# Second layer of a three-layer block: keys transposed among the products of q, query stores on ScalarE's queue, the layer's end re-banked

## The chip, the cores and the metric

The kernel runs on one core of a Trainium2 chip. The core has five engines that run side by side: TensorE (PE, matrix products), VectorE (DVE), ScalarE (ACT), GpSimd (POOL) and SyncE (SP, which here only issues DMAs). The metric is the device time of one execution in microseconds, the median of several runs of the same program.

## What is computed

Three layers over a sequence of L = 1024 tokens of width D = 1024, in float32. The first (sliding-window attention beside a state-space mixer) and the third (a convolution, a second state-space mixer, a gated output) are untouched. The change lies in the second layer, sparse attention, and at the seam to the third:

```python
def odd_layer(hn, rel_bias, w_in, w_out, q_g, k_g):
    q, k, v, gate, qi, ki, wi = split_cols(hn @ w_in, ODD_SPLITS)
    q = rms_norm(q.reshape(bsz, L, C_HEADS, C_HEAD_DIM), q_g)      # 8 heads of 128
    k = rms_norm(k.reshape(bsz, L, C_KV_HEADS, C_HEAD_DIM), k_g)   # 2 heads of 128
    ...
    att = dsa_attention(q, k, v, qi, ki, wi, rel_bias)
    return (att * jax.nn.silu(gate)) @ w_out
```

In `dsa_attention` each query scores all earlier keys with the small index heads `qi`, `ki`, `wi`, keeps the 256 best, and attends to those alone. The layer's result is added to `h`, and the third layer begins with `h = layer_norm(x, ln_emb_g, ln_emb_b)` and one large product of that with `w_in`.

## The kernel before

**Products.** Every float32 operand of a product is split into a high and a low part, and a product of 128 tokens by 512 columns over one slice of the width takes three matrix instructions (`mm3`, L146 to L150). A tile of 128 tokens over the width of 1024 is 8 such triples, 24 instructions (`form1`, L152). Weights arrive in `wraw` by SP, ScalarE copies the high part (L122), GpSimd subtracts for the low part (L123). An instruction's place on its engine is found by a scheduler from priorities, and each engine works through its own list strictly in that order. SP and ScalarE issue DMAs in the same way: one that waits holds up all behind it.

**The k, v and q products** (`phase_b`, L828, from L926 to L958). A loop over eight token tiles makes k and v, 24 instructions each; `head_norm` (L389) copies k out of its bank (L397), squares it (L400), sums on VectorE (L402), forms the root on GpSimd (L168) and multiplies on GpSimd (L406). `keys(tt - 2)` then transposes the normalised k of the tile two back into `kTB` (L933, with a ScalarE scale at L935 and a VectorE split at L936); the last two follow the loop. Then come two halves `ch` of q, eight tiles each, through the same `head_norm`, whose last line (L410) stores the tile to the scratch tensor `d_q` from SP. The copies `qo` have two buffers. While these products run, `TopK` searches for the 256th largest score by bisection in all query blocks: VectorE counts for blocks 2 to 4, ScalarE for blocks 5 to 7 (L1076), 31 steps each, and `finish` (L1083) writes the mask with four long VectorE passes over a scratch tile `cum` (L1118 to L1121).

**The attention** (`DSA`). For each query block and half of the heads, `load` fetches q from `d_q` (L1137), transposes it (`tq`, L1141) and splits it (L1143, L1144). Scores `s` are products of `kTB` and `qTB`. Blocks go in the order 0, 1, 7, 6, 5, 4, 3, 2.

**The layer's end** (L981 to L1002). For each token tile, `out_tile` (L1008) makes columns 512 to 1023 of the output product from the split copies `ms` (L1019, L1020), loads the residual into `hr` (three buffers, L1027 and L1028), adds (L1030) and stores (L1031); `ln_tile` normalises; the tile goes to `d_h0` (L994) and is transposed in two halves into `hnTC`, the stationary or moving operand of the whole third layer. PSUM has eight banks, given out by `k.psum(mm=2, tp=1, sd=3, cy=2)`: the products use the three single banks `sd`, the transposes a two-bank tile `cyt` in one buffer (L995 to L1002).

**The third layer's start** (`phase_c`, L1237). `c_vectors` (L1448) loads short row vectors (L1455 to L1473) and transposes them (L1462, L1470, L1475); then products `pb` and `pa` (two banks `mm`) make the convolution's input, 48 instructions per pair, closed by a sigmoid on ScalarE (L1270) and a product on VectorE (L1271).

## Time and profile before

| | us |
|---|---|
| median of 3 runs | 2135.31 |
| lowest, highest | 2134.58, 2135.98 |
| the profiled execution | 2137.92 |
| its span | 2136.2 |

The profiled execution is one run with the hardware profiler on. Its span, from the first to the last record, is 1.7 us shorter than its own time. TensorE's mean granted clock over the span was 0.955 of full speed. A busy share is an average over stages; what an edit is worth is read in the stage where it lies, from the idle time of the engine that sets the pace there and from what ended that idle time. In the rows below, the name in brackets at the end of a row of a timeline is the idle time just before and the instruction that ended it.

### The profile page before, as it was taken

The numbers are of one execution on the slowest core, as the hardware profiler recorded it, in microseconds if no ns is written. First come the engines' busy times: TensorE is split into PE (matmuls) and PEld (weight loads), VectorE is DVE, ScalarE is ACT, GpSimd is POOL, SyncE is SP. The second block draws the span as 40 slices with busy tenths as digits, with TensorE's granted clock in tenths as the row PEclk, the third lists the DMA queues.
The fourth block names the chain that finished last, engine by engine and source line by source line (L and its number), as shares of the span: only waits on it lengthen the run. The fifth ranks groups of instructions, "written<-read, shape, count | busy, mean of one in ns | idle before, by whom it ended". The sixth has DMA issues, their size and how long they took to land. (4 is left out here: it accounts for less than half of the span.)

```text
span 2136.2 us, 27568 instructions
## 1 busy us (share of the span) xinstructions
PE 1942.1 (91%) x9291; PEld 1571.2 (74%) x9291; DVE 1518.4 (71%) x2995; ACT 846.9 (40%) x1604; POOL 906.7 (42%) x734
## 2 busy tenths in 40 slices
PE   8988899899999998899987799999999659999998
PEld 6777677777788777677856688788888537778786
DVE  8365504674479998598854299999997488857737
ACT  5223326564457885455554221133322411134210
POOL 5567416555322246464566131222232576643204
PEclk9989999999999999899999799999999869999999
DMA  6543332313222212733454132222433445574442
GB/s 196 157 123 106 108 126 86 115 38 114 75 65 70 65 50 81 236 132 119 134 168 156 46 111 78 70 89 80 127 121 106 148 139 171 165 239 175 157 158 99
DMA packets 166694, 256.19 MB, mean 120 GB/s; under 512 B 29078, under 2 KB 77548, under 8 KB 166554
## 3 DMA queue, kind: packets, MB, share of 16 engines
q1 hardware_dynamic: 156330, 236.62, 35.1%
q10 hardware_dynamic: 10224, 17.82, 2.3%
q8 instruction: 73, 1.20, 0.2%
q14 instruction: 67, 0.55, 0.1%
HBM read 185.35 MB, written 75.06 MB: 122 GB/s over the span
## 5 line engine op out<-in xcount | busy, mean ns | idle before, releaser
L123 POOL TENSOR_TENSOR w<-wraw,w 128x512 fp32r<-128x512 f32 (+1 forms) x230 | 313.2, 1376 | 674.7 <-ACT w L122 671.9
L1285 DVE SCALAR_TENSOR_TENSOR cy<-u,cw,cy 128x1024 f32<-128x1024 f32 x232 | 298.7, 1288 | 5.7
L122 ACT ACTIVATE w<-wraw 128x512 fp32r<-128x512 f32 (+1 forms) x230 | 141.4, 622 | 191.5 <-DMA wraw<-in_w_in_dram 53.3
L149 PE MATMUL mm<-hnTC,w 128*128 128x512 f32 (+1 forms) x336 | 131.6, 392 | 0.0
L150 PE MATMUL mm<-hnTC,w 128*128 128x512 f32 (+1 forms) x336 | 131.5, 391 | 0.0
L148 PE MATMUL mm<-hnTC,w 128*128 128x512 f32 (+1 forms) x336 | 131.5, 391 | 0.0
L1165 POOL TENSOR_TENSOR lgB<-lgB,sc 128x1024 f32<-128x1024 f32 (+5 forms) x48 | 84.4, 1788 | 75.7 <-DMA lgB<-d_T 73.1
L148 PE MATMUL mm<-w,ms 128*128 128x512 f32 x256 | 105.1, 410 | 10.1 <-ACT ms L1019 9.3
L150 PE MATMUL mm<-w,ms 128*128 128x512 f32 x256 | 105.5, 412 | 7.3 <-POOL ms L1020 6.9
L1076 ACT ACTIVATE tkj<-sc,tks 128x896 bf16<-128x896 f32 (+2 forms) x93 | 96.4, 1038 | 26.1 <-DVE tks L1072 23.8
L149 PE MATMUL mm<-w,ms 128*128 128x512 f32 x256 | 103.2, 403 | 1.4 <-POOL w L123 1.2
L168 POOL TENSOR_TENSOR hr<-hm,mhalf 128x2 f32<-128x2 f32 (+2 forms) x40 | 46.8, 1170 | 89.4 <-DVE hm L403 57.8
L148 PE MATMUL mm<-w,hnTA 128*128 128x512 f32 (+1 forms) x192 | 73.1, 384 | 7.8 <-DVE qo L406 7.8
L148 PE MATMUL mm<-hnTB,w 128*128 128x512 f32 (+2 forms) x208 | 78.4, 377 | 0.7 <-ACT hnTB L172 0.7
L149 PE MATMUL mm<-w,hnTB 128*128 128x512 f32 x192 | 77.5, 404 | 0.9 <-POOL w L123 0.9
L149 PE MATMUL mm<-hnTB,w 128*128 128x512 f32 (+2 forms) x208 | 78.1, 376 | 0.0
L150 PE MATMUL mm<-hnTB,w 128*128 128x512 f32 (+2 forms) x208 | 78.1, 375 | 0.0
L148 PE MATMUL mm<-w,hnTB 128*128 128x512 f32 x192 | 77.7, 406 | 0.0
L150 PE MATMUL mm<-w,hnTB 128*128 128x512 f32 x192 | 77.3, 403 | 0.0
L149 PE MATMUL mm<-w,hnTA 128*128 128x512 f32 (+1 forms) x192 | 73.3, 382 | 0.3 <-POOL w L123 0.3
L150 PE MATMUL mm<-w,hnTA 128*128 128x512 f32 (+1 forms) x192 | 73.3, 383 | 0.0
L148 PEld LDWEIGHTS mm<-hnTC,w 128*128 128x128 f32 (+1 forms) x336 | 61.6, 183 | 14.6
(609 smaller groups left out, 5899.2 us busy)
## 6 DMA issues: line engine op xcount, KB each, us to landing
wraw<-in_w_in_dram SPq DMA_DIRECT2D x56, 256.0 KB
wraw<-in_od_w_in_dram SPq DMA_DIRECT2D x48, 256.0 KB
wraw<-in_ev_w_in_dram SPq DMA_DIRECT2D x32, 256.0 KB
wraw<-in_w_in_dram SPq DMA_DIRECT2D x64, 128.0 KB
wraw<-in_w_out_dram SPq DMA_DIRECT2D x32, 256.0 KB
ld<-d_cs SPq DMA_DIRECT2D x16, 512.0 KB
hr<-h SPq DMA_DIRECT2D x24, 256.0 KB
d_T<-d_row SPq DMA_DIRECT2D x8, 576.0 KB
```

Source lines behind the costliest of these rows:

```text
L122: nc.scalar.activation(t[:, 0, :o], raw[:, :o], AF.Copy)
L123: nc.gpsimd.tensor_tensor(t[:, 1, :o], raw[:, :o], t[:, 0, :o].bitcast(F32), op=ALU.subtract)
L148: mm(out, aH, bH, start=start, stop=False)
L149: mm(out, aH, bL, start=False, stop=False)
L150: mm(out, aL, bH, start=False, stop=stop)
L168: self.nc.gpsimd.tensor_tensor(out, ms, self.mhalf[:, :n], op=ALU.pow)
L1076: S.activation(self.junk(n), sc[b], AF.Sign, bias=cand[:, i:i + 1], accum_out=cnt[:, i:i + 1])
L1165: G.tensor_tensor(lg[:, :n], lg[:, :n], self.masks[b], op=ALU.add)
L1285: V.scalar_tensor_tensor(py if i < 30 else y, u[:, i:i + L], cw[:, ct, i:i + 1], py, op0=ALU.mult, op1=ALU.add)
```

## The change

- `keys` is no longer called among the k, v products. It follows each q tile of the first half, and its transposes are tied behind that tile's last product (`k.last`, set in `mm3`) by `tc.issue_after`. The eight normalised k tiles wait in the two `rl` tiles (four of them) and in the tile `cum` (the other four), so the first `cum` pass of `TopK.finish` comes after the last key transpose.
- The stores to `d_q` leave SP. `head_norm` takes a callback `store`, called right after its ScalarE copy: tile t's store is issued by ScalarE after the copy of tile t + 1, and ScalarE waits there for GpSimd's multiplication of tile t.
- At the layer's end the output products use the two `mm` banks, the transposes the three `sd` banks, one half tile each (`to_hnT`, L175).
- `c_vectors` moves from ahead of the third layer's first products to behind the first pair of them, tied with `issue_after`. Lines after L147 are shifted by one to a few.

```diff
@@ mm3
-        mm(out, aL, bH, start=False, stop=stop)
+        self.last = mm(out, aL, bH, start=False, stop=stop)
@@ head_norm(..., o=None, store=None)
     if leave:
-        S.activation(o[:, :n], ps, AF.Copy)
-        ps = o[:, :n]
+        S.activation(o, ps, AF.Copy)
+        if store is not None:
+            store()
+        ps = o
@@ k, v and q products
-    def keys(tt, kn):
+    kn = [xp.tile([P, 512], F32, tag="rl", name="kn", bufs=2) for _ in range(2)]
+    kn.append(xp.tile([P, L], F32, tag="cum", name="kn", bufs=1))
+    def kraw(tt):
+        return kn[min(tt // 2, 2)][:, (tt % 2 if tt < 4 else tt - 4) * 256:][:, :256]
+    def keys(tt):
         pt = k.tp()
-        for j in range(2):
-            T.transpose(pt[:, j * P:(j + 1) * P], kn[:, j * P:(j + 1) * P], k.ident)
+        with tc.issue_after(k.last.ins):
+            for j in range(2):
+                T.transpose(pt[:, j * P:(j + 1) * P], kraw(tt)[:, j * P:(j + 1) * P], k.ident)
...
-        if tt > 1:
-            keys(tt - 2, kns[tt - 2])
-        if tt % 2 == 0:
-            kn2 = xp.tile([P, 512], F32, tag="rl", name="kn", bufs=2)
-        kns.append(head_norm(k, gp, ps[:, :256], 2, 128, None, True, kn2[:, tt % 2 * 256:tt % 2 * 256 + 256]))
-    for tt in range(NT - 2, NT):
-        keys(tt, kns[tt])
+        head_norm(k, gp, ps[:, :256], 2, 128, None, True, kraw(tt))
+    store = None
...
-            head_norm(k, gp, ps, 4, 128, d_q[tt * P:(tt + 1) * P, ch * 512:ch * 512 + 512], True)
+            if ch == 0:
+                keys(tt)
+            o = head_norm(k, gp, ps, 4, 128, None, True, None, store)
+            store = partial(nc.scalar.dma_start, d_q[tt * P:(tt + 1) * P, ch * 512:ch * 512 + 512], o)
+    store()
@@ the layer's end
-        h = out_tile(k, mo, op, tt, 1, [mix], wo, x, hout, bank="sd")
+        h = out_tile(k, mo, op, tt, 1, [mix], wo, x, hout)
...
-        cy = k.pp.tile([P, L], F32, tag="cy", name="cyt", bufs=1)
-        for hf in range(2):
-            c = cy[:, hf * 512:hf * 512 + 512]
-            for kk in range(4):
-                T.transpose(c[:, kk * P:(kk + 1) * P], h[:, (hf * 4 + kk) * P:(hf * 4 + kk + 1) * P], k.ident)
-            hs = slice(hf * 4, hf * 4 + 4)
-            k.split_bank(c.rearrange("p (k t) -> p k t", k=4), hnC[:, 0, hs, tt * P:(tt + 1) * P],
-                         hnC[:, 1, hs, tt * P:(tt + 1) * P])
+        k.to_hnT(h, hnC, tt, "sd")
@@ phase_c
-    c_vectors(k, up, cw, sw, dtx, sng)
...
                 k.form2(pa, hnT, th * 512, w, KT, m * P)
+                if j + th + m == 0:
+                    with tc.issue_after(k.last.ins):
+                        c_vectors(k, up, cw, sw, dtx, sng)
```

**SP's list at the q products.** `wraw` is a weight load, `lgB` a bias load of the attention. Before:

```order
L110 DMA wraw<-in_od_w_in_dram 128x512 x34
L410 DMA d_q<-qo 128x512 x6
L110 DMA wraw<-in_od_w_out_dram 128x512 x4
L410 DMA d_q<-qo 128x512
L110 DMA wraw<-in_od_w_out_dram 128x512 x3
L410 DMA d_q<-qo 128x512
L110 DMA wraw<-in_od_w_out_dram 128x512
L410 DMA d_q<-qo 128x512 x3
L1137 DMA qf<-d_q 128x512
L1163 DMA lgB<-d_T 128x128 x4
```

Now:

```order
L111 DMA wraw<-in_od_w_in_dram 128x512 x34
L111 DMA wraw<-in_od_w_out_dram 128x512 x8
L1138 DMA qf<-d_q 128x512
L1164 DMA lgB<-d_T 128x128 x4
L1138 DMA qf<-d_q 128x512
```

The eleven stores ahead of the first query load, and the five behind it, are gone from this list and stand in ScalarE's.

**VectorE's list where the mask of block 2 is finished** (`kTB<-` is the split of a key tile, `cum<-` the first passes of the mask, `tks_` and `hm` small steps of the search and of `head_norm`). Before:

```order
L936 SCALAR_TENSOR_TENSOR kTB<-tp,bg,kTB 128x2x128
L1107 TENSOR_TENSOR tks_7495<-tks_7495 128x3
L1072 TENSOR_SCALAR tks_7516<-tks_7516 128x1
L403 TENSOR_SCALAR hm<-hm 128x2
L1115 TENSOR_SCALAR tkj_7496,tks_7495<-sc_5062,tks_7495 128x384
L1116 TENSOR_SCALAR eq<-sc_5062,tks_7495 128x384
L1080 TENSOR_TENSOR tks_7542<-tks_7542 128x1
L1117 TENSOR_SCALAR tks_7495<-tks_7495 128x1
L1118 SCALAR_TENSOR_TENSOR cum<-mone,eq 128x384
```

Now:

```order
L1116 TENSOR_SCALAR tkj_7529,tks_7528<-sc_5066,tks_7528 128x896
L1118 TENSOR_SCALAR tks_7528<-tks_7528 128x1
L1081 TENSOR_TENSOR tks_7541<-tks_7541 128x1
L1119 SCALAR_TENSOR_TENSOR cum<-mone,eq 128x384
L1082 COPY_PREDICATED tks_7541<-tks_7541 128x1
L1120 SCALAR_TENSOR_TENSOR cum<-cum,tks_7494,eq 128x384
L1073 TENSOR_SCALAR tks_7541<-tks_7541 128x1
L946 SCALAR_TENSOR_TENSOR kTB<-tp,bg,kTB 128x2x128
L1121 TENSOR_TENSOR cum<-cum,tkj_7495 128x384
```

The `cum` passes of blocks 2, 3 and 4 stood behind the sixth of the eight key splits and now stand around the eighth, with those of blocks 5, 6 and 7 close behind; the last of block 7 stands directly ahead of the first query's split, as before.

**TensorE's list at the end of the layer** (its first row is the last of 24 products `pa`). Before:

```order
L150 MATMUL pa<-hnTC,w 128x512
L999 MATMUL cyt<-ident,hr 128x128 x4
L1462 MATMUL tp<-ident,rows 128x36 x8
L999 MATMUL cyt<-ident,hr 128x128 x4
L1470 MATMUL tp<-ident,rows_11079 128x5 x6
L1470 MATMUL tp<-ident,rows_11088 128x5 x6
L999 MATMUL cyt<-ident,hr 128x128 x4
L1475 MATMUL tp<-ident,rows_11098 128x8
L999 MATMUL cyt<-ident,hr 128x128 x16
```

Now:

```order
L151 MATMUL pa<-hnTC,w 128x512
L182 MATMUL tph<-ident,hr 128x128 x4
L1465 MATMUL tp<-ident,rows 128x36 x4
L182 MATMUL tph<-ident,hr 128x128 x4
L1465 MATMUL tp<-ident,rows 128x36 x4
L1473 MATMUL tp<-ident,rows_11184 128x5 x6
L1473 MATMUL tp<-ident,rows_11193 128x5 x6
L149 MATMUL pb<-hnTC,w 128x512
```

Of the last transposes of `hr` seven groups of four stood between the first pair of products and the second; now two do, and the one of L1475 stands inside the second pair. Between the last product of the output (`mm<-w,ms`) and these rows stand 36 products `pb` and `pa` and one group of `cyt` before, 34 products and two groups of `tph` now. In SP's list the load of `conf_conv_w` (L1455) stood directly behind the store of tile 6's sum (L1031) and now stands behind the store of the normalised tile 6 (L994); the two loads of the residual of tile 7 (L1027, L1028) stood behind the loads of the row vectors and now stand ahead of them, behind the store of the normalised tile 4.

## Rows read from the trace of the kernel before

**Rows 1.** The page, busy time by engine: us, share of the span, instructions.

```profile
PE 1942.1 (91%) x9291; PEld 1571.2 (74%) x9291; DVE 1518.4 (71%) x2995; ACT 846.9 (40%) x1604; POOL 906.7 (42%) x734
```

**Rows 2.** Stretches of the span: length, busy time by engine, granted clock, DMA.

```profile
core 0: us, PE busy (x) PEld busy (x) DVE busy (x) ACT busy (x) POOL busy (x), PEclk, DMA share, GB/s
1160.00:1180.00 20.00, 8.69 (x48) 6.81 (x46) 5.96 (x15) 5.08 (x9) 3.98 (x4) 0.68 0.32 109
1200.00:1300.00 100.00, 100.00 (x443) 82.81 (x442) 72.84 (x62) 16.69 (x26) 20.51 (x16) 1.00 0.26 82
```

**Rows 3.** TensorE's waits from 734 to 875 us: total, times, longest.

```profile
PE tp L933 <- POOL kn L406: 8.3, 2, 5.2
```

**Rows 4.** TensorE in time, k, v and q products: start, length, line, [idle <-releaser].

```profile
733.80 0.39 PE L150 MATMUL mm<-w,hnTB 128*128 128x512 f32 x1
739.39 0.69 PE L933 MATMUL tp<-ident,kn 128*128 128x128 f32 x2 [5.20 <-POOL kn L406]
...
837.69 0.39 PE L149 MATMUL mm<-w,hnTB 128*128 128x512 f32 x1
...
848.57 0.39 PE L149 MATMUL mm<-w,hnTB 128*128 128x512 f32 x1
857.42 1.12 PE L1141 MATMUL tq<-ident,qf 128*128 128x128 f32 x4 [8.46 <-DMA qf<-d_q]
...
872.60 0.22 PE L148 MATMUL s<-kTB,qTB 128*128 128x128 f32 x1
```

**Rows 5.** SP's queue in time, at the end of the products of q.

```profile
839.55 14.23 SPq L410 DMA_DIRECT2D d_q<-qo  x3
853.88 0.38 SPq L1137 DMA_DIRECT2D qf<-d_q  x1
```

**Rows 6.** Issuing one DMA from ScalarE (stores of d_gate), ns min/median/max.

```profile
L922 ACTq DMA_DIRECT2D d_gate<-gtB x16: 326/326/327, 609.1 to 718.5; - x16
```

**Rows 7.** Two stretches of the k, v and q products, columns of rows 2.

```profile
734.20:800.00 65.80, 57.50 (x243) 46.77 (x244) 65.61 (x281) 56.39 (x121) 26.98 (x28) 0.92 0.14 41
800.00:854.00 54.00, 48.06 (x209) 38.51 (x207) 47.17 (x122) 31.13 (x56) 35.66 (x26) 0.99 0.23 79
```

**Rows 8.** VectorE in time, the last block's top-k ends, first query follows.

```profile
847.68 2.28 DVE L1118 TENSOR_TENSOR_SCAN cum<-mone,eq 128x1024 f32<-128x1024 f32 x1
...
853.06 0.93 DVE L1121 TENSOR_SCALAR sc<-cum 128x1024 f32<-128x1024 f32 x1
...
859.29 0.75 DVE L1144 SCALAR_TENSOR_TENSOR qTB<-tq,bg,qTB 128x512 fp32r<-128x512 f32 x1 [1.23 <-ACT qTB L1143]
```

**Rows 9.** ScalarE's copy of a tile of q, and GpSimd's last step on it.

```profile
812.61 0.58 ACT L397 ACTIVATE qo<-mm 128x512 f32<-128x512 f32 x1
...
817.06 1.04 POOL L406 TENSOR_TENSOR qo<-qo,hr 128x512 f32<-128x512 f32 x1
```

**Rows 10.** TensorE in time, end of the second layer.

```profile
1154.14 0.39 PE L150 MATMUL mm<-w,ms 128*128 128x512 f32 x1
...
1172.55 0.61 PE L1462 MATMUL tp<-ident,rows 36*128 36x36 f32 x4 [8.93 <-DMA rows<-in_b_glu_dram]
...
1193.69 0.79 PE L148 MATMUL pb<-hnTC,w 128*128 128x512 f32 x1 [2.69 <-ACT stg L1270]
```

**Rows 11.** Residual adds (tiles 5, 6), GpSimd's end of tile 5's layer norm.

```profile
1140.64 0.68 DVE L1030 TENSOR_TENSOR hr<-mm,hr 128x512 f32<-128x512 f32 x1
...
1155.80 0.69 DVE L1030 TENSOR_TENSOR hr<-mm,hr 128x512 f32<-128x512 f32 x1 [4.93 <-DMA hr<-h]
...
1146.40 1.74 POOL L1229 TENSOR_TENSOR hr<-hr,bbC 128x512 f32<-128x512 f32 x1
```

**Rows 12.** SP's queue in time: loads of the row vectors.

```profile
1156.88 0.30 SPq L1455 DMA_DIRECT2D rows<-in_conf_conv_w_dram  x1
...
1165.21 0.25 SPq L1457 DMA_DIRECT2D rows<-in_conf_ln_g_dram  x1
...
1169.56 0.29 SPq L1458 DMA_DIRECT2D rows<-in_b_glu_dram  x1
```

More of the change, by code (lines that the diff above doesn't have):

```diff
@@ L1 @@
 from contextlib import ExitStack
+from functools import partial
 import math
@@ L386, in phase_a, with head_norm @@
     return hnT, sB
-def head_norm(k, pool, ps, nh, dh, dst, leave=False, o=None):
+def head_norm(k, pool, ps, nh, dh, dst, leave=False, o=None, store=None):
     nc = k.nc
@@ L394, in head_norm @@
     if o is None:
-        o = pool.tile([P, 512], F32, tag="qo", name="qo", bufs=2)
+        o = pool.tile([P, 512], F32, tag="qo", name="qo", bufs=2)[:, :n]
     if leave:
-        S.activation(o[:, :n], ps, AF.Copy)
-        ps = o[:, :n]
+        S.activation(o, ps, AF.Copy)
+        if store is not None:
+            store()
+        ps = o
     sq = pool.tile([P, 512], F32, tag="sq", name="sq", bufs=1)
@@ L405, in head_norm @@
     k.rstd(r[:, :nh], m[:, :nh], nh)
-    (G if leave else V).tensor_tensor(o[:, :n].rearrange("p (h d) -> p h d", h=nh),
+    (G if leave else V).tensor_tensor(o.rearrange("p (h d) -> p h d", h=nh),
                                       ps.rearrange("p (h d) -> p h d", h=nh),
@@ L409, in head_norm @@
     if dst is not None:
-        nc.sync.dma_start(dst, o[:, :n])
+        nc.sync.dma_start(dst, o)
     return o
@@ L937, in keys @@
                                op0=ALU.mult, op1=ALU.subtract)
-    kns = []
     for tt in range(NT):
```

## The prediction, made before the changed kernel ran

> **What bounds the kernel now.** I read the page first, then the windows, then TensorE's waits and its timeline at the two places that the change touches, and last the lists that release it there. TensorE is busy for 1942.1 of 2136.2 us [rows 1], so an edit is worth the TensorE idle time (or half-clock time) that it removes, where nothing else takes its place. Behind the second place TensorE is full: 100.00 of 100.00 us from 1200 on [rows 2]. What is gained before 1200 therefore reaches the end; nothing later can absorb it. The sum is made against the profiled execution, 2137.92 us, which is 2.6 above the median 2135.31; I take the 2.6 off at the end. From no change a measurement here tells about 0.2%, 4.3 us.
>
> First place, the k, v and q products. TensorE stops for the keys: it stood 5.20 us at 739.39, 8.3 in two stops [rows 3, 4], because the k of two tiles back had not yet passed `head_norm` on GpSimd. It stops again 8.46 us before the query transpose at 857.42, for a load of q [rows 4]. Nothing was slow in that load. SP stood 14.23 us in three stores of q, each waiting for GpSimd's multiplication, and the load was issued directly behind them, at 853.88 [rows 5]. The first score product starts at 872.60 [rows 4].
>
> Second place, the layer's end. The last output product is at 1154.14, the second pair of the third layer's products begins at 1193.69 [rows 10], and of the 20 us from 1160 TensorE works 8.69, at a granted clock of 0.68 [rows 2]. In there lie a wait of 8.93 us for a row vector and four serial rounds through the one `cyt` tile.
>
> **The first place, step by step.** Three chains end at the first score product.
>
> *TensorE.* 48 product starts take 10.88 us (837.69 to 848.57), 0.2267 each [rows 4]. By the engine's list 486 products lie between the first key transpose of before and the first score product, 110.2 us. The four query transposes are 1.12 us on record, just behind a stop [rows 4]; 16 key transposes and those four at that price are 5.6. From 734.0, where the last product ahead of the first stop leaves the array, this gives 849.8.
>
> *VectorE.* It was busy 65.61 of 65.80 us and then 47.17 of 54.00 [rows 7], 112.8 us of work up to the end of block 7's mask at 853.06 + 0.93 = 854.0 [rows 8]. Without its 7.0 us of idle time the same work would end at 847.0. The edit adds none, but moves the masks of blocks 2 to 4 behind the last key transpose. I hold the end where it is, at 854.0: the idle time is what the moved passes will use up. The first query's split adds 0.75 [rows 8], which gives 854.8, call it 855.
>
> *ScalarE.* 16 stores at 0.326 us, the price of its stores of `d_gate` [rows 6], are 5.2 us. The wait before each is bounded by `head_norm`'s chain: the copy at 812.61 to the end of GpSimd's multiplication at 818.10 is 5.5 us [rows 9], against a tile time of 24 x 0.2267 = 5.4. So a store that stands one tile later finds its data about ready. ScalarE had 23 us free in the second stretch [rows 7], which hides the 5.2. If the cover is gone, the 5.2 fall on the search.
>
> VectorE ends last, at 855 instead of 872.6: **17.6 us**. The bounds: 22.8 if both engines run gap-free (849.8), 12.4 if the stores' 5.2 us fall on VectorE's chain.
>
> The query's load I book as no longer late: with the stores on ScalarE it stands behind weight loads alone in SP's list. Here the Trainium skill speaks against the change: "DMA: Bandwidth & Descriptors", section "Issuing engines are not separate DMA queues", says that DMAs of all issuing engines run on the same 16 engines, so spreading them saves only the issue time. By that rule the move would be worth those issues alone; the rows show SP waiting 14.23 us, not the 16 engines, which were busy 0.23 of that stretch [rows 7].
>
> **The second place, step by step.** Now 34 products follow the last output product, 7.7 us, then four groups of `hr` transposes and 20 small ones. At 1.12 us a group [rows 4] and 0.61 for each four of the small ones [rows 10] that is 4.5 and 3.1, so the second pair could begin at 1154.4 + 15.3 = 1169.7. Two things can hold it.
>
> *The row vectors.* The load of `conf_conv_w` now follows the store of the normalised tile 6. Tile 5 took from its sum at 1140.64 to GpSimd's end at 1148.14, 7.5 us [rows 11]. Tile 6's sum came at 1155.80, late by 4.93 for its residual load [rows 11]; one tile after tile 5 it would be at 1148.1. `conf_conv_w` to the next load behind it took 8.3 us, the last of the row loads to its transpose 3.0 [rows 10, 12]; four issues between add 1.2. So the rows are there at 1148.1 + 7.5 + 8.3 + 1.2 + 3.0 = 1168.1 at best, 1175.8 if tile 6 is as late as before. I take the middle, 1172, since the residual loads of tiles 6 and 7 moved ahead. One group of `hr` transposes and the small ones follow, 1.1 + 3.1, so the second pair begins at 1176.2.
>
> *Tile 7.* Its sum can follow its product at 1154.6, its layer norm ends 7.5 later at 1162.1, so its transposes do not wait longer than the rows. With single banks the four serial rounds of before are gone.
>
> The gain is 1193.7 - 1176.2 = **17.5 us**; the bounds are 21.4 (rows at 1168.1, the pair at 1172.3) and 13.7 (rows at 1175.8, the pair at 1180.0). The clock falls in the wait as it did before, and I book nothing for it. The two `mm` banks for three `sd` at the output products I book at nothing: each bank is released by one sum of 0.68 us [rows 11], against 5.4 us for a tile's 24 products. If a sum waits for its residual as tile 6's did, 4.9 us are lost once; the lower bound holds that.
>
> **The sum.** 2137.92 - 17.6 - 17.5 = 2102.8 for a profiled run, less 2.6: **2100 us**. With the bounds of both places, 26.1 to 44.2 us, this case reaches from 2091 to 2109.
>
> **The rivals.**
>
> *A. The load stays late.* If the transfer engines and not the list held the query, the query's transpose stays at 857.42. It takes 1.12 and the list puts 23 products behind it, 5.2 us, so the scores start at 863.7, a gain of 8.9 at the first place: 2109. For it: the load landed within 3.5 us of its issue, so little of its lateness was the transfer's, but the stores still share the engines with it [rows 4, 5]. Against it: SP's own 14.23 us. Chance 0.05. (It is the case of the rule of the Trainium skill named above.)
>
> *B. VectorE pays for the moved masks.* The last four passes over 1024 columns took 6.3 us [rows 8]; blocks 2 to 4 have 384 + 512 + 640 = 1536 columns, 9.5 us. If these find no idle time behind the last key split, the scores start at 864.5, a gain of 8.1: 2110. For it: VectorE was full until 800. Against it: 6.8 us free after [rows 7]. Chance 0.22.
>
> *C. The row vectors are later than I think.* With weight loads between them and tile 6's store late, 1172 can become 1181; the second place gives 9: 2109. Against it: the rows' loads were only 13 us long in all [rows 12]. Chance 0.15.
>
> *D. Slower: ScalarE's list blocks.* Behind each waiting store stand the copy that frees a bank, the square, and the search's signs for blocks 5 to 7. If each of 16 stores holds ScalarE 2.9 us on average, its issue included, the search ends 16 x 2.9 = 47 us later, the scores start at 902, 29 later than before, and with the second place's 17.5 the time is 2147. It decides from (17.6 + 17.5 + 4.3) / 16 = 2.5 us per store. Against it: chain and tile time are equal to 0.1 us. Chance 0.05.
>
> *E. Nothing comes through.* The scores start early but wait for bias loads or masks, and the end of the layer waits for a new load: about 2134. Against it: full windows later [rows 2]. Chance 0.03.
>
> **How the numbers follow.** The forecast has 0.50, A 0.05, B 0.22, C 0.15, D 0.05, E 0.03. B and C together would give 2118. The range is 2090 to 2120: it holds the forecast with its bounds, A, B, C and B with C, and leaves out D and E and what lies beyond the bounds. Faster: 0.50 + 0.05 + 0.22 + 0.15 = 0.92; same 0.03; slower 0.05.
>
> **What would show it.** Right: no TensorE wait at the key transposes, or under 3 us in all; no wait for `qf`; the first score product 12 to 25 us earlier; ScalarE's waits at the stores below 1 us each; the second pair of the third layer's products 34 to 42 us earlier in the trace than 1193.69. Wrong: a TensorE wait for `kTB`'s bank or the mask as long as those removed; the search's last sign later than before; a wait at the row vectors above 9 us; or idle TensorE in the third layer's full windows.

## The result, and the profile after

The changed kernel takes **2118.72 us**, the median of 4 runs (2112.16 to 2122.16), against 2135.31: a ratio of 0.9919, with a 95% interval of 0.9894 to 0.9943. It is faster by 16.6 us, where 35 were forecast. 2118.72 lies within the range 2090 to 2120, close to its upper end; the direction was right and the size was not. Two later timings of the same program, beside other runs of the kernel before, gave 0.9931 (0.9916 to 0.9946) and 0.9934 (0.9918 to 0.9950). The profiled execution below took 2112.16 us, the shortest of its four, with a span of 2110.3.

The page's busy times answer to [rows 1]. The instructions of TensorE are the same 9291; they take 10.5 us less, at a mean granted clock of 0.962 for 0.955.

```profile
PE 1931.6 (92%) x9291; PEld 1564.4 (74%) x9291; DVE 1513.9 (72%) x2995; ACT 845.0 (40%) x1604; POOL 903.8 (43%) x734
```

**The first place.** The waits of TensorE from 734 to 875 us answer to [rows 3]. The waits for `kn` and for the query load are gone. In their place are a wait of 8.9 us of the first score product for the query's split on ScalarE, and small ones for weight halves (`w`), which a TensorE that no longer stops now catches up with.

```profile
PE s L149 <- ACT qTB L1144: 8.9, 1, 8.9
PE s L149 <- DVE stB L1178: 3.3, 1, 3.3
PE mm L149 <- ACT w L123: 3.2, 1, 3.2
PE mm L150 <- POOL w L124: 2.0, 2, 1.1
PE tp L943 <- DVE kTB L946: 1.6, 1, 1.6
```

TensorE's timeline there answers to the last two rows of [rows 4]. The query's transpose comes 9.9 us earlier and no longer waits for its load; the first score product comes 10.3 earlier in its trace, and stands for 8.93 us ahead of that.

```profile
847.52 0.60 PE L1142 MATMUL tq<-ident,qf 128*128 128x128 f32 x4
...
862.32 0.47 PE L149 MATMUL s<-kTB,qTB 128*128 128x128 f32 x1 [8.93 <-ACT qTB L1144]
```

SP's queue, which answers to [rows 5], shows that the query's load is early, at 827.43. Behind it SP stands for 29.31 us in the loads of the attention's bias tiles; they end at 857.2, right behind the last mask (856.35); the profile has the last of them waiting 12.7 us for that mask's last pass (`sc`).

```profile
827.43 0.37 SPq L1138 DMA_DIRECT2D qf<-d_q  x1
827.91 29.31 SPq L1164 DMA_DIRECT2D lgB<-d_T  x4
857.38 0.32 SPq L1138 DMA_DIRECT2D qf<-d_q  x1
```

ScalarE's timeline has the stop (rows marked ACTq are stores that ScalarE issues; their second number is how long the pair took from the first issue on, the wait between the two included).

```profile
846.11 4.67 ACTq L400 DMA_DIRECT2D d_q<-qo  x2
850.89 0.60 ACT L398 ACTIVATE qo<-mm 128x512 f32<-128x512 f32 x1 [6.80 <-POOL qo L409]
...
858.37 2.62 ACTq L400 DMA_DIRECT2D d_q<-qo  x2
861.09 0.60 ACT L398 ACTIVATE qo<-mm 128x512 f32<-128x512 f32 x1 [5.87 <-DMA d_q<-qo]
861.58 0.68 ACT L1144 ACTIVATE qTB<-tq,bg 128x512 fp32r<-128x512 f32 x1
```

The split at 861.58 had its transpose since 848. It stands behind the copy at 861.09, that copy waits until a store has landed (`qo` has two buffers), and that store waited for GpSimd's multiplication; the pair's second store, issued at 860.66, stands ahead of the copy in ScalarE's list as well. Before, such a copy stood ahead of the split too, but it was over before the query's transpose (857.42):

```profile
855.82 0.60 ACT L397 ACTIVATE qo<-mm 128x512 f32<-128x512 f32 x1 [7.38 <-DMA d_q<-qo]
...
858.57 0.69 ACT L1143 ACTIVATE qTB<-tq,bg 128x512 fp32r<-128x512 f32 x1 [1.50 <-PE tq L1141]
```

VectorE's timeline, which answers to [rows 8], closes the chain: GpSimd waits for the small steps `hm` of `head_norm`, and the first of them stands at 853.82 behind two long `cum` passes.

```profile
849.57 3.01 DVE L1119 TENSOR_TENSOR_SCAN cum<-mone,eq 128x1024 f32<-128x1024 f32 x1
852.61 1.28 DVE L1120 SCALAR_TENSOR_TENSOR cum<-cum,tks,eq 128x1024 f32<-128x1024 f32 x1
853.82 0.68 DVE L405 TENSOR_REDUCE hm<-sq 128x4 f32<-128x512 f32 x1
...
855.66 0.69 DVE L1122 TENSOR_SCALAR sc<-cum 128x1024 f32<-128x1024 f32 x1
...
862.30 0.75 DVE L1145 SCALAR_TENSOR_TENSOR qTB<-tq,bg,qTB 128x512 fp32r<-128x512 f32 x1 [3.93 <-ACT qTB L1144]
```

The stretches answer to [rows 2, 7], in their columns. From 734.2 to 854 TensorE works 112.49 us, 105.56 before. Behind it, in the 20 us from 860, the clock is at the lower of its two levels for nearly all of the time (0.55).

```profile
734.20:800.00 65.80, 60.23 (x263) 48.57 (x262) 59.13 (x269) 61.11 (x129) 28.74 (x32) 0.97 0.16 47
800.00:854.00 54.00, 52.26 (x233) 42.51 (x231) 52.34 (x116) 24.98 (x45) 33.11 (x24) 1.00 0.27 88
...
840.00:860.00 20.00, 13.38 (x61) 10.72 (x60) 17.32 (x29) 3.70 (x6) 9.39 (x9) 0.94 0.21 71
860.00:880.00 20.00, 13.67 (x55) 11.32 (x56) 13.15 (x55) 12.02 (x30) 8.54 (x9) 0.55 0.68 208
880.00:900.00 20.00, 16.46 (x83) 12.91 (x81) 11.72 (x46) 8.51 (x24) 5.61 (x4) 0.91 1.07 315
...
1160.00:1180.00 20.00, 13.43 (x60) 10.47 (x59) 4.26 (x12) 5.09 (x7) 2.52 (x2) 0.74 0.19 65
1200.00:1300.00 100.00, 100.00 (x443) 82.79 (x442) 91.79 (x78) 20.88 (x33) 28.61 (x23) 1.00 0.32 97
```

**The second place.** TensorE's timeline, to [rows 10]: from the last output product to the second pair it takes 19.6 us, 39.5 before. The wait for the row vectors is 3.81 us instead of 8.93, and the four serial rounds are gone.

```profile
1151.08 0.39 PE L151 MATMUL mm<-w,ms 128*128 128x512 f32 x1
...
1164.32 0.41 PE L1465 MATMUL tp<-ident,rows 36*128 36x36 f32 x4 [3.81 <-DMA rows<-in_b_glu_dram]
1166.39 1.11 PE L182 MATMUL tph<-ident,hr 128*128 128x128 f32 x4 [1.67 <-POOL hr L1230]
...
1170.67 0.79 PE L149 MATMUL pb<-hnTC,w 128*128 128x512 f32 x1
```

SP's queue, to [rows 12], has `conf_conv_w` 1.1 us and `b_glu` 10.5 us behind the last output product, 2.7 and 15.4 before. 4.83 us of that are two weight loads that wait.

```profile
1152.16 0.29 SPq L1458 DMA_DIRECT2D rows<-in_conf_conv_w_dram  x1
...
1156.12 4.83 SPq L111 DMA_DIRECT2D wraw<-in_w_in_dram  x2
...
1161.62 0.25 SPq L1461 DMA_DIRECT2D rows<-in_b_glu_dram  x1
```

### The profile page after: what moved, and what is told of

Read it like the earlier page. It is cut to its first block, busy times and chain, and to the rows that moved or that the text cites. A ratio compares the mean times of both kernels' runs of the same rounds, so it can differ in the third digit from the quotient of the medians.

```text
span 2110.3 us, 27572 instructions
## 1 busy us (share of the span) xinstructions
PE 1931.6 (92%) x9291; PEld 1564.4 (74%) x9291; DVE 1513.9 (72%) x2995; ACT 845.0 (40%) x1604; POOL 903.8 (43%) x734
## 5 line engine op out<-in xcount | busy, mean ns | idle before, releaser
L149 PE MATMUL mm<-w,hnTB 128*128 128x512 f32 x192 | 76.0, 397 | 3.2 <-ACT w L123 3.2
L150 PE MATMUL mm<-w,hnTB 128*128 128x512 f32 x192 | 75.7, 394 | 2.0 <-POOL w L124 2.0
L151 PE MATMUL mm<-w,hnTB 128*128 128x512 f32 x192 | 75.4, 393 | 0.0
```

Of the source, the lines that this page charges most:

```text
L149: mm(out, aH, bH, start=start, stop=False)
L150: mm(out, aH, bL, start=False, stop=False)
L151: self.last = mm(out, aL, bH, start=False, stop=stop)
```

## Three stretches of every run

The experiments are easiest to read by one table. Each trace has its own zero: the first split of `v` on VectorE (`vB`, 732.14 in the trace before, 729.61 after). From it to the first score product `s` is the stretch "products"; from there to the last output product (`mm<-w,ms`) is "attention"; from there to the second pair `pb` is "seam". "Mask" is the end of the last mask, from the same zero. All in us. The ratio is to the runs of the kernel before that were taken beside it. Each row's stretches are from one trace; the three traces of the change differ by up to 2.5 us in the products and 3.4 in the attention, so less than that between two rows says little.

| run | mask | products | attention | seam | sum | median | ratio, 95% interval |
|---|---|---|---|---|---|---|---|
| before | 121.9 | 140.5 | 281.5 | 39.5 | 461.6 | | |
| the change | 126.7 | 132.7 | 288.8 | 19.6 | 441.1 | 2118.72 | 0.9919, 0.9894 to 0.9943 |
| r1_after (the change again) | 129.2 | 135.2 | 292.2 | 19.2 | 446.6 | 2118.04 | 0.9931, 0.9916 to 0.9946 |
| r3_after (the change again) | 129.1 | 135.0 | 290.1 | 19.3 | 444.5 | 2116.44 | 0.9934, 0.9918 to 0.9950 |
| e1_end_only | 121.8 | 139.7 | 282.0 | 17.4 | 439.0 | 2114.58 | 0.9915, 0.9884 to 0.9945 |
| r4_end_only (again) | 121.8 | 140.0 | 281.9 | 17.3 | 439.2 | 2113.11 | 0.9922, 0.9901 to 0.9942 |
| e2_front_only | 129.1 | 135.1 | 289.5 | 30.0 | 454.5 | 2127.83 | 0.9978, 0.9964 to 0.9991 |
| e3_stores_sp | 126.6 | 132.0 | 281.9 | 15.8 | 429.7 | 2105.58 | 0.9865, 0.9836 to 0.9895 |
| r2_stores_sp (again) | 126.6 | 131.9 | 282.9 | 15.8 | 430.7 | 2107.03 | 0.9892, 0.9872 to 0.9911 |
| e4_keys_old | 121.8 | 129.9 | 293.8 | 19.4 | 443.1 | 2113.16 | 0.9906, 0.9883 to 0.9928 |
| e6_stores_pool | 127.0 | 133.4 | 292.5 | 15.9 | 441.8 | 2117.57 | 0.9928, 0.9913 to 0.9943 |
| e7_no_banks | 126.7 | 132.7 | 291.8 | 29.4 | 453.9 | 2128.28 | 0.9974, 0.9960 to 0.9988 |
| e8_early_vectors | 129.0 | 135.0 | 289.1 | 19.6 | 443.6 | 2119.94 | 0.9932, 0.9910 to 0.9955 |
| e10_gate_late | 126.7 | 132.6 | 288.7 | 15.9 | 437.3 | 2113.05 | 0.9912, 0.9885 to 0.9939 |
| e11_sp_gate_late | 126.7 | 132.2 | 286.6 | 15.9 | 434.7 | 2107.88 | 0.9886, 0.9867 to 0.9905 |
| e12_sp_lag3 | 122.2 | 134.7 | 286.1 | 16.2 | 437.0 | 2110.75 | 0.9897, 0.9880 to 0.9915 |
| e13_sp_lag3_late | 122.2 | 134.7 | 288.1 | 15.7 | 438.5 | 2113.57 | 0.9923, 0.9895 to 0.9952 |
| e14_split_dve | 129.8 | 132.5 | 294.4 | 19.3 | 446.1 | 2118.33 | 0.9947, 0.9926 to 0.9967 |

Sum and median go together to within some 4 us: the three stretches hold nearly all that the versions differ by. The change shortens the products by 5 to 8 us, **lengthens the attention by 7 to 11**, and shortens the seam by 20.

The attention falls behind within its first 60 us. The rows are the products, the first 60 us of the attention and its rest, for before, the change and e3, in the columns of [rows 2]:

```profile
732.14:872.60 140.46, 122.79 (x516) 99.07 (x515) 119.33 (x416) 95.52 (x189) 72.47 (x64) 0.93 0.21 65
872.60:932.60 60.00, 51.69 (x256) 41.02 (x255) 48.84 (x159) 31.45 (x72) 29.99 (x16) 0.91 0.73 227
932.60:1154.14 221.54, 203.18 (x1025) 161.22 (x1025) 166.04 (x388) 120.10 (x232) 131.17 (x91) 0.99 0.44 144
...
729.61:862.32 132.71, 117.08 (x515) 94.89 (x513) 119.47 (x414) 92.42 (x186) 66.30 (x60) 0.97 0.21 66
862.32:922.32 60.00, 50.30 (x231) 39.70 (x232) 46.66 (x148) 29.53 (x69) 33.51 (x19) 0.84 0.72 228
922.32:1151.08 228.76, 209.85 (x1068) 167.33 (x1067) 171.75 (x411) 127.70 (x248) 130.06 (x92) 0.99 0.44 145
...
730.98:862.94 131.96, 119.84 (x515) 96.73 (x513) 119.71 (x414) 92.23 (x186) 66.33 (x60) 0.95 0.19 63
862.94:922.94 60.00, 51.74 (x260) 41.23 (x261) 50.32 (x161) 33.41 (x77) 33.58 (x19) 0.91 0.74 237
922.94:1144.87 221.93, 202.85 (x1034) 161.22 (x1033) 170.32 (x398) 123.22 (x239) 130.48 (x92) 0.99 0.45 150
```

In those 60 us TensorE gets through 231 instructions in the change (222 and 217 in its repeats), and 256 before and 260 in e3; in the rest all three do some 4.6 to 4.7 a us. It is idle 1.4 us longer there than before (2.35 and 2.65 in the repeats), and its granted clock is 0.84 (0.83 and 0.82) for 0.91. So most of the lag is time at the lower clock. Over all the traces the two go together: the clock of these 60 us is 0.80 to 0.86 in the twelve whose attention takes 286.6 us or more, 0.89 to 0.91 in the six with 286.1 or less. And over products and attention together TensorE is idle 44.2 us in the change (47.0 and 43.3 in its repeats), 44.3 before, 39.5 in e3: the change moved TensorE's stops, it did not shorten them in sum.

## The experiments

Kernels of one group ran on the same chip and share their runs of the kernel before (the texts on record say "call" for such a group).

**First group: the parts apart.** e1 has the second place alone (the layer's end as changed; keys, stores and `head_norm` as before), e2 the first place alone (keys and stores as changed, the end as before). e3 is the whole change with the stores back on SP, e4 the whole change with the keys back among the k, v products.

```diff
 e3
-            o = head_norm(k, gp, ps, 4, 128, None, True, None, store)
-            store = partial(nc.scalar.dma_start, d_q[tt * P:(tt + 1) * P, ch * 512:ch * 512 + 512], o)
-    store()
+            head_norm(k, gp, ps, 4, 128, d_q[tt * P:(tt + 1) * P, ch * 512:ch * 512 + 512], True)
 e4
+        if tt > 1:
+            keys(tt - 2, kns[tt - 2])
...
-            if ch == 0:
-                keys(tt)
```

> Only the end of the layer is changed (single banks for the transposes, two banks for the products, late row vectors); keys and stores of q as before. Theory A (the end is worth about 20 us, as in the one trace of the changed kernel, and the spread of the changed kernel's times comes from the stores on ScalarE): 2115 us, between 2112 and 2118, runs within 2 us of each other. Theory B (the end is fragile, its loads are what makes the runs differ, and it is worth 10 to 12 on average): 2123 us with runs some 8 us apart.

> Only the first place is changed (keys among the products of q, stores of q from ScalarE); the end of the layer as before. Theory A: the scores start some 10 us earlier but the attention ends only 3 to 4 us earlier, so 2131 us, between 2127 and 2137, with runs 5 to 10 us apart. Theory B: 2125 us, runs within 2 us.

> The whole change but for the stores of q, which stay in SP's list. Theory A: no ScalarE wait at a store, TensorE waits for the first query's load again (some 8 us or more), the scores start between 862 and 872; 2112 to 2117 us, runs within 3 us. Rival (the stores on ScalarE are what the first place needs, and the keys alone only move TensorE's wait): 2120 us or above, the scores not before 870.

> The whole change but for the keys, which are transposed among the products of k and v as before. Theory A: the two stops at the key transposes (8 us) are back, ScalarE still waits at the stores, runs are 5 to 10 us apart; 2115 to 2122 us, about the whole change. Rival (the moved keys, which push the masks of blocks 2 to 4 back, are what delays the first query): the first query's split does not wait on ScalarE, and the time is 2110 or below with little spread.

e1 alone takes 18.7 us off (2133.31 to 2114.58), as much as the whole change. So the first place, for which 17.6 us were booked, is worth nothing on top of the second, or a little less than nothing. e2 takes 5.5 us off, and the table shows where from: not from products and attention, which together are 2.5 us longer than before, but from its seam, 30.0 for 39.5, although the code of the seam is that of before. The scheduler had sorted SP's list there anew (the residual loads of tile 7 now follow the load of `conf_ln_g`; they followed those of `b_glu` and `ssm_conv_b`). TensorE's timeline of e2 shows a wait of 3.37 us at the row vectors, for 8.93, and the serial rounds still there, with a second pair that begins 17.3 us behind the first transpose of row vectors, for 21.1:

```profile
1169.29 0.61 PE L1470 MATMUL tp<-ident,rows 36*128 36x36 f32 x4 [3.37 <-DMA hr<-h]
...
1177.74 1.09 PE L1007 MATMUL cyt<-ident,hr 128*128 128x128 f32 x4 [1.30 <-DVE hnTC L174]
1180.24 1.12 PE L1007 MATMUL cyt<-ident,hr 128*128 128x128 f32 x4 [1.41 <-DVE hnTC L174]
...
1186.63 0.80 PE L149 MATMUL pb<-hnTC,w 128*128 128x512 f32 x1 [2.69 <-ACT stg L1278]
```

e3 is the fastest, and below both of its forecasts (2112 and 2120). With the stores on SP the load of q is late again, and TensorE waits for it, 6.24 us. It still starts its scores at the same place as the change, and its attention is as short as that of before. TensorE's timeline, ScalarE's and the stretches of e3:

```profile
854.91 1.12 PE L1140 MATMUL tq<-ident,qf 128*128 128x128 f32 x4 [6.24 <-DMA qf<-d_q]
...
862.94 0.33 PE L149 MATMUL s<-kTB,qTB 128*128 128x128 f32 x1 [0.58 <-ACT qTB L1142]
```

```profile
861.71 0.60 ACT L398 ACTIVATE qo<-mm 128x512 f32<-128x512 f32 x1 [5.21 <-DMA d_q<-qo]
862.20 0.68 ACT L1142 ACTIVATE qTB<-tq,bg 128x512 fp32r<-128x512 f32 x1
```

```profile
860.00:880.00 20.00, 14.40 (x67) 11.40 (x66) 12.60 (x54) 11.96 (x30) 9.71 (x10) 0.74 0.72 228
880.00:900.00 20.00, 18.14 (x97) 14.65 (x96) 15.75 (x56) 9.74 (x26) 9.42 (x6) 1.00 1.07 322
```

So the first query's split stands behind the same waiting copy, although ScalarE has no store in its list. From the end of the last mask the scores start 5.30 us later in e3 and in r2, 5.96 in all three traces of the change: ScalarE's stores are worth 0.7 us there. What differs is where TensorE stands. In e3 it stops ahead of the query's transpose and then has products to do until the split is ready; in the change it has done them, and stands 8.93 us directly ahead of the scores.

e4 has no stop ahead of its first scores, which come earliest of all (129.9), and its attention is the second longest (293.8). Its waits of TensorE from 734 to 875 show the stop further on among the scores, at the softmax's small tile `stB`, for 7 us:

```profile
PE s L149 <- DVE stB L1171: 8.8, 3, 7.0
```

Its last mask ends as early as before (121.8). Its time, 2113.16, lies between its two forecasts.

**Second group: the second place in two, and a third queue.** e7 has the whole change without the new banks at the end, e8 without the late vectors. In e6 GpSimd issues the stores, directly behind its own multiplication.

```diff
 e6
-            o = head_norm(k, gp, ps, 4, 128, None, True, None, store)
-            store = partial(nc.scalar.dma_start, d_q[tt * P:(tt + 1) * P, ch * 512:ch * 512 + 512], o)
-    store()
+            o = head_norm(k, gp, ps, 4, 128, None, True)
+            nc.gpsimd.dma_start(d_q[tt * P:(tt + 1) * P, ch * 512:ch * 512 + 512], o)
 e7
-        h = out_tile(k, mo, op, tt, 1, [mix], wo, x, hout)
+        h = out_tile(k, mo, op, tt, 1, [mix], wo, x, hout, bank="sd")
-        k.to_hnT(h, hnC, tt, "sd")
+        cy = k.pp.tile([P, L], F32, tag="cy", name="cyt", bufs=1)
...
 e8
+    c_vectors(k, up, cw, sw, dtx, sng)
...
-                if j + th + m == 0:
-                    with tc.issue_after(k.last.ins):
-                        c_vectors(k, up, cw, sw, dtx, sng)
```

> The whole change, with the stores of q issued by GpSimd right behind its own multiplication, so that neither ScalarE nor SP waits for it. Theory A (the stores on ScalarE take back what the keys gain; the copy that splits the first query stands behind a copy that waits for a store to land): no ScalarE wait of several us ahead of the first query's split, scores within 3 us of the end of block 7's mask, 2098 to 2108 us. Theory C (the masks' end and the bias loads that need its memory set the attention's start, wherever the stores stand): as the run with the stores on SP or no better, 2104 to 2110, first product with the gate (mixB) no more than 5 us earlier than before.

> The whole change without the new banks: output products in the three single banks, transposes in the one two-bank tile; row vectors late. If the serial rounds through the one tile are most of the second place, the gap from the last output product to the second pair is 30 us or more and the time 2126 to 2132 us; if the row vectors' wait is most of it, the gap is 22 to 26 us and the time 2120 to 2124.

> The whole change with the row vectors early, ahead of the third layer's first products, as before; new banks. If the banks are most of the second place: gap 21 to 25 us, 2118 to 2123 us. If the row vectors are: 28 us or more, 2126 us or above.

> The changed kernel itself once more, beside the same runs of the kernel before as the other three. Theory A: 0.989 to 0.994 of before, and ScalarE again waits for the landing of a store just ahead of the first query's split. If the trace shows another wait there, the first trace was not typical.

e8 has the seam of the whole change, 19.6, and its time (0.9932 beside 0.9931). e7 has 29.4, where e2, without either part, had 30.0, and e2's time. So, with the first place changed, **the banks are all that the second place adds**, some 10 us of seam, and the late vectors are worth nothing, alone or on top. Beside keys and stores as before, where both together take the seam from 39.5 to 17.4 (e1), the two were not run apart. In e7 the serial rounds stand at 2.5 us each, as in e2.

In e6 ScalarE's list has no store in it, yet TensorE waits 7.0 us for the same split. The copies ahead of it still wait for a `qo` that GpSimd has not yet multiplied or stored (6.94 us at the last of them), and GpSimd is late because its input `hm` comes late. So ScalarE's own issuing is not what makes the stop. By the rows the order of VectorE's list is one of its causes; no run changed that order alone. e6 was no faster than the change, and slower than both of its forecasts (at most 2110).

**Third group: what else could hold the attention.** In e10 and e11 the loads of the gate (`mixB`), which SP issued ahead of the next bias tiles, are tied behind those; e10 is the change, e11 has the stores on SP. In e12 the keys stay three tiles back, the last three among q, so that `cum` isn't used for them and the masks end as early as before; the stores are on SP. e13 is e12 with the late gate loads.

```diff
 e10, e11, e13
-                nc.sync.dma_start(lg[:, :n], dap(self.d_T, h * P * 1152 + 127 + P * (7 - b), [[1151, P], [1, n]]))
+                self.ld = nc.sync.dma_start(lg[:, :n], dap(self.d_T, h * P * 1152 + 127 + P * (7 - b), [[1151, P], [1, n]]))
...
-        k.nc.sync.dma_start(mx, self.d_gate[:, hs, ts_])
+        with k.tc.issue_after(self.ld.ins):
+            k.nc.sync.dma_start(mx, self.d_gate[:, hs, ts_])
 e12, e13
-            if ch == 0:
-                keys(tt)
+            if ch == 0 and tt < 3:
+                keys(tt + 5)
```

> The whole change, and each load of the gate (mixB<-d_gate, 256 KB) is tied on SP behind the bias loads of the unit that follows, so that block 7's first biases (512 KB each) are no longer behind 12 gate loads. Theory D (the attention's start is bound by that burst of loads, which begins when the memory under it comes free and so ate the earlier scores): GpSimd's first addition to block 7's bias 8 us or more earlier against the first split of v than the 167 to 169 us of the change and of before, the attention's last product with the gate 6 us or more earlier, 2108 to 2113 us. Theory A (ScalarE's stores alone eat it): no change, 2116 to 2120 us.

> The whole change with the stores of q in SP's list, and the gate loads tied as in the run before. Theory D: 2098 to 2103 us, some 3 to 6 below the run with the stores on SP alone. Theory A: no change against that run, 2104 to 2107.

> The stores of q in SP's list; keys transposed three tiles back and the last three among the q products, in the two rl tiles alone, so that cum is not needed and the masks of blocks 2 to 4 keep their place. If the delayed masks cost the first place its gain: block 7's mask ends 4 to 5 us earlier against the first split of v (122 instead of 126.7 us), 2098 to 2103 us. If not: 2104 to 2108 us, as with the stores on SP alone.

> Both together: stores on SP, keys three tiles back, gate loads late. Theory D: the best of all, 2094 to 2101 us. If the burst does not matter: as the run before it.

The gate loads aren't it. GpSimd's first bias add of block 7 came at 157.3 and 157.4 us from the zero in e10 and e11, for 167.2 in the change and 162.1 in e3, and the attention stayed at 288.7 and 286.6. The last product with the gate ended 351.9 us from the zero in e10, within the 348.9 to 354.3 of the change. e10's time, 2113.05, reaches the upper end of theory D's range all the same, by a shorter seam (15.9). Nor are the masks alone: e12 has them 4.4 us earlier than e3, and its products and attention are no shorter (2.7 and 4.2 us longer). e11, e12 and e13 (2107.88, 2110.75, 2113.57) all came out above the ranges on record for a gain, at most 2103.

**Fourth group: the split off ScalarE.** Open until here was whether the place of the first query's split in ScalarE's list is the cost. e14 is the change with that query's high part made by VectorE. e3, the change and e1 ran again beside it.

```diff
-        S.activation(qT[:, 0], src, AF.Copy, scale=kg[:, 0:1])
+        if (b, kv) == (DORD[0], 0):
+            V.tensor_scalar(qT[:, 0], src, kg[:, 0:1], None, op0=ALU.mult)
+        else:
+            S.activation(qT[:, 0], src, AF.Copy, scale=kg[:, 0:1])
```

> The whole change, but the first query's high part is written by VectorE (0.7 us) instead of ScalarE, so ScalarE's stores are no longer ahead of it. If ScalarE's list is the cause: the scores start within 3 us of block 7's mask, TensorE's stop there is 4 to 5 us shorter, and the time is 4 us or more below the whole change in the same call. If the attention's start uses up earlier scores: the stop is shorter but the time within 2 us of the whole change, and the lost time shows as TensorE waits in the first four units.

> The stores of q in SP's list, as in the earlier run, again: 0.984 to 0.989 of before, and 8 us or more below the whole change in the same call, if ScalarE's stores are what the first place lost; else within 4 us of it.

> The changed kernel for comparison in the same call: 0.991 to 0.994 of before.

> The end of the layer alone, for comparison in the same call: 0.990 to 0.993 of before; if the first place of the change is worth nothing or less, no more than 2 us above the whole change, or below it.

e14's time is that of the change (2118.33 and 2116.44). The stop did not get shorter, so the run does not tell what it costs; the wait changed its name and went on. TensorE's timeline of e14 has it for VectorE, then again at the low part, 9.3 us in all, for 8.9, 8.9 and 6.8 in the traces of the change.

```profile
865.33 0.47 PE L149 MATMUL s<-kTB,qTB 128*128 128x128 f32 x1 [5.68 <-DVE qTB L1145]
...
870.11 0.69 PE L151 MATMUL s<-kTB,qTB 128*128 128x128 f32 x2 [3.66 <-DVE qTB L1148]
```

In this group e3's version (2107.03, 2106.18 to 2108.05) beats the change (2116.44) by 9 us, and their intervals don't overlap. It beats the end alone (2113.11) by 6 us; in neither group do the single runs of the two overlap (2106.18 to 2108.05 against 2108.70 to 2119.28 here; 2098.72 to 2108.74 against 2111.39 to 2117.72 in the first), though the intervals of their ratios overlap in both. So the key move is worth some 6 to 9 us to this kernel if the stores stay on SP. It is the version to keep.

## Why the prediction was wrong in size

**The second place held.** 17.5 us were forecast, with bounds of 13.7 and 21.4. The seam shrank by 19.9 in the trace, and alone it brought 18.7 and 18.6 us. The row vectors come 13.2 us behind the last output product, against 17.6 by the forecast: `conf_conv_w` follows tile 6's store closely, since tile 6's sum waits no longer (4.93 before). That the total came out so close is in part luck: I spoke of row vectors and banks as two parts, and with the first place changed only the banks count. With the banks as changed, the vectors' place in TensorE's list made no difference (e8). And 9.5 us of the 39.5 were a matter of the old order of SP's list, which the first edit moves by itself (e2, and e7 with 29.4); I had booked nothing of the kind.

**The first place failed**, 17.6 forecast and nothing found. What it set out to remove is gone: the key stops (8.3 us) and the wait for the query's load (8.46). Three steps failed, and the last one decides.

*"ScalarE: a store that stands one tile later finds its data about ready."* The price of a store was right (0.33 us each), and the first eight made ScalarE wait for nothing that shows. From 834 on each of the next six held it, for 3.5, 2.9, 2.0, 4.0, 3.2 and 2.0 us. From the seventh tile on, the start of a copy and the end of its multiplication lie 7.5 to 12.7 us apart. I compared `head_norm`'s chain at an undisturbed tile (5.5 us) with a tile's time, and did not ask what VectorE does to that chain once long `cum` passes stand ahead of its small steps. The wait of ScalarE's copies for landed stores isn't new, 12.0 us in four now and 13.5 in five before; what is new is that the first query's split stands behind 15 of the 16 copies, for 13 before. That goes with the moved keys and not with the stores: it is 15 in e3 as well, and 13 in e4. In short, the load was made early, and the split behind it stayed late.

*"VectorE ends last, at 855."* It does not end last, and I had held its end where it was. From the zero the last mask ends 4.8 to 7.3 us later than before. It does so in every run in which keys wait in `cum` (126.6 to 129.8), and not in those in which none do (e4, e12 and e13, 121.8 to 122.2). That is rival B's mechanism, at half to three quarters of its price of 9.5. And the scores follow it by 6.0 us, where I had booked 0.75 for the split: between them stand the last steps of `head_norm`, GpSimd's multiplication, a store and the copy behind it. With the stores on SP it is 5.3, so ScalarE's stores are the smaller part by far. Together they leave 5 to 8 of the 17.6 us at the first score product.

*The sum took an earlier first score for an earlier end.* This is the step that made the time wrong. The scores start 5 to 8 us earlier from the zero, and the attention takes all of it back. It is 7 to 11 us longer in all three traces of the change, and most of that falls in its first 60 us, at a granted clock of 0.82 to 0.84 for 0.91. In the change TensorE stood 7 to 9 us directly ahead of the scores; before, it stood 8.46 us ahead of the query's transpose, 15 us earlier. I had taken the removed stops off the sum, with no term for a new stop or for the clock behind it. So rival E, to which I gave 0.03, describes the first place: the scores are early and what follows isn't. Its price, 2134, was wrong, because I had tied it to a loss at the second place too. The argument against it, full windows from 1200 on, says nothing of the stretch between 873 and 1150.

Two slips in the working change nothing: 16 x 2.9 in rival D is 46.4 and not 47, and the 1.12 us for four transposes, taken just behind a stop, was measured at the lower clock; where TensorE had not stopped four took 0.60 (847.52).

**The other rivals.** A fell: the load comes 20 us ahead of the transpose. That was the case of the rule of the Trainium skill, "DMA: Bandwidth & Descriptors", section "Issuing engines are not separate DMA queues". Its conclusion, that spreading the stores gains little, agrees with the runs as far as it goes (the kernel is 9 us faster with them on SP); its reason, the shared transfer engines, isn't the one at work here, since these were busy 0.21 of the time from 840 to 860, where the stop begins. D's mechanism is there in small, six waits of 17.5 us in all where 39 would have made the kernel slower, and doesn't decide. C fell.

**What stays open** is why the attention is 282 to 283 us long with the stores on SP (e3, r2), and the seam 15.8, but 289 to 294 (and mostly 19) with the same keys and the stores issued by ScalarE or GpSimd. The traces show where the attention's time goes, the lower clock of its first 60 us and up to 6 us more idle time; that TensorE's stop directly ahead of the scores is what brings the lower clock there was not tested, since no run with the moved keys took that stop away and left the rest. Candidates that the runs ruled out as the only cause are ScalarE's issuing (e6), the gate loads (e10, e11) and the late masks (e12). e14 did not rule out the stop, which it kept. Another one remaining is the order of the lists: the scheduler writes them anew with each edit, and in the traces TensorE's instructions stand in another order in e3 than in the change, in the attention above all. Versions with the stores on SP and other orders have 286.1 to 288.1 (e11, and with other keys e12 and e13), so the order may well be worth some microseconds by itself. The same order of the attention with another queue was not run.

## What to carry to other kernels

An engine's list is a queue for everything in it: moving a store from a DMA-only engine to a computing one moves its wait there too (here six waits of 2.0 to 4.0 us), so list what stands behind the store in its new place. Then ask whether that wait is the one that ends last: here the split was nearly as late with the stores back on SP, since the copy ahead of it waits for a stored tile whichever engine issues the store. An earlier start is worth only what the next stage hands on: cost it by when that stage ends, and add up the waiting engine's idle time over both stages, which here did not fall at all (44.3 and 44.2 us). Test each part of a change alone, because one part may hold the whole gain and another may take from it. Where a scheduler orders the lists, an edit at one place also moves instructions at another (here 9.5 us at a seam whose code had not changed), so compare the order far from the edit too.

## What the runs showed that I had not expected

- The three first runs of the kernel before lay within 1.4 us of each other. In the four later groups single runs reached from 2125.47 to 2140.90, while the medians of the groups stayed within 2131.64 to 2133.31. A difference of less than some 5 us can't be read from three runs, and so not from one trace either.
- After TensorE's 8.93 us stop the granted clock of the 20 us from 860 was 0.55; in e3, which stopped 6.24 us and then 0.58, it was 0.74 in the same 20 us of its trace, and 1.00 in the next.
- In the 20 us from 880 the DMA share reads 1.07 at 315 GB/s in the change and 1.07 at 322 in e3: full transfer engines did not tell the slower attention from the faster one.
